# Conformer stage of a four-layer trunk: the whole depthwise convolution as 32x32 tiles on TensorE, modulation rows on VectorE

## The chip, the cores and the metric

The kernel runs on one core of a Trainium2 chip. The metric is the device time of one execution in microseconds (us), taken as the median of several runs. The engines are called as in the profile: PE is TensorE (PEld its weight loads), DVE is VectorE, ACT is ScalarE, POOL is GpSimd and SP is SyncE, which here issues the loads of weights.

## The reference, cut to what matters

A sequence of 256 tokens with 2048 channels passes four layers; the first one is a Conformer convolution module. Every sub-layer is gated and modulated by six vectors (shift, scale and gate of the mixer, then of the feed-forward network) that a per-layer projection, called adaLN, makes from one conditioning vector `c`.

```python
# each sub-layer f:  x <- x + gate * RMSNorm_post(f(RMSNorm_pre(x) * (1 + scale) + shift))
def _conv_module(h, w_in, dw_w, dw_b, ln_g, ln_b, w_out):
    a, gate = jnp.split(h @ w_in, 2, axis=-1)
    z = _causal_dwconv(a * jax.nn.sigmoid(gate), dw_w, dw_b)   # 31 taps for each channel
    z = jax.nn.silu(_layer_norm(z, ln_g, ln_b))
    return z @ w_out
```

All of it is in float32. The change touches only this module and the way in which the first layer's six modulation vectors are computed.

## The kernel before, in words

**Layout.** Channels lie on the 128 partitions, in 16 blocks (`KT` = 16, `P` = 128, `T` = 256 tokens). A matrix product in float32 is made of three products of a rounded part `hi` and a remainder `lo`: ACT writes `hi` (L121) and DVE writes `lo` (L123) for each weight. Weights arrive as items of 1 MB, 128x2048, in one list that SP loads in order.

**The input projection.** It runs in six steps, called s0 to s5 here, by the table `STEPS`: each takes some of the 16 input blocks (`nk` of them from `k0` on) for the output blocks `j0` to `j1`. Steps s0 to s2 add to all sixteen, s3 and s4 finish blocks 0 to 7, and s5 makes blocks 8 to 15 complete from eight input blocks. The matmuls are L756 to L758 (`ps_cin`). The function `gather` adds a result to `pair` (L665), and at a block's last step multiplies it by the sigmoid of its gate (L671).

**The convolution.** Eight blocks are convolved on DVE: 30 instructions each (L685), one per tap, two blocks at a time. The other eight (`PE_BLOCKS`) go over PE: four delayed copies of the block are made by matmuls with an identity (L713), copied out by ACT (L715), and 32 matmuls with diagonal weights add the taps (L730); the diagonals `zt` are made by DVE (L724) and ACT (L728), and ACT adds the bias (L733). The order in which these pieces are recorded is written out (`conv(dve, taps_dve, 8)` after each item of the last steps, then a loop over the rest).

**LayerNorm.** It runs over channels, that is over partitions. PE sums the blocks with a matrix of ones (L644 for the mean, L633 for the squares, one matmul of 128 columns for each block). DVE then forms `r_ln` (L783 to L786), takes the mean off all blocks (L789), multiplies each by `r_ln` (L792); ACT applies SiLU (L793), and the pair L424 and L425 splits the result into `uc`, the operand of the output projection (`ps_cout`, L522 to L524).

**Modulation.** A block of 128 values of a modulation vector can be made in two ways. As a *row*: DVE multiplies a 128x2048 item with the broadcast vector `cb` and sums along the line (L350). As *columns*: PE multiplies four items with `cz` (L364, 32 columns each, four tiles side by side in `ada`), DVE transposes the sums (L371) and PE adds them up (L378). Of the first layer's 96 blocks, 52 are made from columns before and 28 from rows, beside the 16 of the last gate, which come later, from rows, in both kernels. After the last step, 16 column items are used in the convolution's tail (`early_cols`) and some more in the output projection (`COLS_COUT`).

**What sets the order.** A scheduler puts the recorded instructions on each engine in an order that is then fixed; an engine runs its own in that order and waits at semaphores. `high_priority` and `issue_after` bend the order. Items wait in pools of four buffers: `raw` for weights and `cols` for early modulation items, and a load is issued when its buffer is free.

## Time and profile before

| what | value |
|---|---|
| median of 3 runs | 2378.56 us (2376.98 to 2380.26) |
| the profiled execution | 2376.87 us |
| its span, first to last instruction | 2375.2 us |
| granted clock of PE, mean | 0.992 |
| PE busy | 2318.7 us (98%) |
| DVE busy | 1772.2 us (75%) |
| ACT busy | 1212.4 us (51%) |
| DMA, mean | 256 GB/s over the span |

The profiled execution is 1.69 us below the median. The stages that the change touches end at about 466 us of the span: s0 begins at 29.6, s1 at 61.2, s2 at 95.1, s3 at 149.7, s4 at 183.7 and s5 at 211; the tail of the convolution runs from 266.7 to 352.4, LayerNorm up to 368.8, and the output projection up to 466.

A row of the table of windows gives the window, its length, then for PE, PEld, DVE, ACT and POOL the busy time and, in brackets, the number of instructions, then the granted clock, the share of DMA and its rate. A row of the timeline gives start, length, engine, operation and, in square brackets, the idle time before it with what ended it.

### The profile page before, as it was taken

The page shows a single profiled execution, that of the slowest core. Times are in us where ns is not written, and L with a number is a line of the kernel's source. Part 1 is how long each engine was busy: PE and PEld are TensorE (multiplying, and loading weights), DVE is VectorE, ACT ScalarE, POOL GpSimd, SP SyncE. Part 2 cuts the span into 40 slices and gives each one's busy share as a digit, 9 for nine tenths or more (in the row PEclk, how much of TensorE's full clock was granted, in tenths as well). Part 3 has the DMA queues.
Part 4 walks back from the last instruction along what each step waited for, and adds up shares of the span by engine and source line. Part 5 has one row for each costly group of instructions (what it writes and reads, how often), then busy time and mean ns, then how long its engine had stood idle before and what let it go on. Part 6 is the DMA issues. An engine that isn't in the chain of part 4 may idle for free.

```text
span 2375.2 us, 34238 instructions
## 1 busy us (share of the span) xinstructions
PE 2318.7 (98%) x13516; PEld 1955.8 (82%) x13516; DVE 1772.2 (75%) x2554; ACT 1212.4 (51%) x1909; POOL 16.8 (1%) x43
## 2 busy tenths in 40 slices
PE   6999998999999999999999999999999999999998
PEld 5888746788878888888878888888888888888886
DVE  3779998778878888888877877756887466645665
ACT  5334465555534554345565576655554455544543
POOL 0000000000000000000000000000000000000000
PEclk9999998999999999999999999999999999999999
DMA  9878778657799878988946756563778555555553
GB/s 387 344 311 322 299 222 309 265 216 276 291 310 348 303 279 316 362 288 298 345 174 258 283 216 227 168 227 121 286 280 275 193 190 193 189 185 196 193 199 121
DMA packets 86577, 609.30 MB, mean 257 GB/s; under 512 B 10064, under 2 KB 10128, under 8 KB 13456
## 3 DMA queue, kind: packets, MB, share of 16 engines
q1 hardware_dynamic: 84800, 601.84, 69.2%
q0 software_dynamic: 1472, 4.23, 0.6%
q8 instruction: 106, 1.74, 0.3%
q10 hardware_dynamic: 144, 1.05, 0.1%
q14 instruction: 55, 0.45, 0.1%
HBM read 604.94 MB, written 2.13 MB: 256 GB/s over the span
## 4 chain that ended last, share of the span: by engine, by line
PE 95%; DMA 2%; DVE 1%; ACT 1%; issue 0%; SPq 0%; DVEq 0%; ACTq 0%
PE ps_fb L410 14%; PE ps_fa L410 14%; PE ps_fa L412 7%; PE ps_fb L412 7%; PE ps_fo L524 7%; PE ps_fo L523 7%; PE ps_fo L522 6%; PE ps_cin L756 3%; PE ps_cin L758 3%; PE ps_r L410 2%; PE ps_cin L757 2%; PE ada L364 2%; PE ps_r L412 1%; PE ps_q L410 1%; PE ps_cout L522 1%; PE ps_k L410 1%
## 5 line engine op out<-in xcount | busy, mean ns | idle before, releaser
L123 DVE TENSOR_TENSOR lo<-raw,hi 128x1024 fp32r<-128x1024 f32 (+1 forms) x760 | 914.3, 1214 | 398.7 <-ACT hi L121 395.5
L121 ACT CAST hi<-raw 128x1024 fp32r<-128x1024 f32 (+1 forms) x760 | 784.9, 1042 | 807.4 <-PE ps_fa L410 195.4
L410 PE MATMUL ps_fa<-h,hi 128*128 128x512 f32 x1408 | 356.4, 393 | 0.4 <-ACT hn L486 0.4
L410 PE MATMUL ps_fb<-h,hi 128*128 128x512 f32 x1408 | 354.9, 392 | 0.0
L350 DVE CUSTOM_DVE_ANT_0 raw<-raw,cb 128x2048 f32<-128x2048 f32 x140 | 319.6, 2284 | 30.6 <-DMA raw<-in_adar 30.5
L410 PEld LDWEIGHTS ps_fa<-h,hi 128*128 128x128 f32 x1408 | 252.9, 189 | 45.7 <-DVE h L488 0.6
L410 PEld LDWEIGHTS ps_fb<-h,hi 128*128 128x128 f32 x1408 | 252.5, 189 | 44.2
L523 PE MATMUL ps_fo<-lo,u 128*128 128x512 f32 x704 | 274.6, 390 | 4.1 <-DVE lo L123 4.1
L524 PE MATMUL ps_fo<-hi,u 128*128 128x512 f32 x704 | 274.6, 390 | 0.0
L522 PE MATMUL ps_fo<-hi,u 128*128 128x512 f32 x704 | 273.7, 390 | 0.0
L412 PEld LDWEIGHTS ps_fa<-h,lo 128*128 128x128 f32 x1408 | 193.7, 190 | 15.1 <-DVE lo L123 0.5
L412 PEld LDWEIGHTS ps_fb<-h,lo 128*128 128x128 f32 x1408 | 193.7, 190 | 14.7
L412 PE MATMUL ps_fa<-h,lo 128*128 128x256 f32 x1408 | 198.3, 282 | 0.1
L412 PE MATMUL ps_fb<-h,lo 128*128 128x256 f32 x1408 | 198.2, 282 | 0.0
L523 PEld LDWEIGHTS ps_fo<-lo,u 128*128 128x128 f32 x704 | 132.6, 188 | 32.1 <-DVE lo L123 4.6
L756 PE MATMUL ps_cin<-h,hi 128*128 128x256 f32 x512 | 148.4, 293 | 7.3 <-ACT hi L121 7.2
L524 PEld LDWEIGHTS ps_fo<-hi,u 128*128 128x128 f32 x704 | 132.5, 188 | 27.7
L522 PEld LDWEIGHTS ps_fo<-hi,u 128*128 128x128 f32 x704 | 132.6, 188 | 27.1
L758 PE MATMUL ps_cin<-h,lo 128*128 128x256 f32 x512 | 145.2, 288 | 1.1 <-DVE lo L123 1.1
L757 PE MATMUL ps_cin<-h,hi 128*128 128x256 f32 x512 | 146.0, 287 | 0.0
L756 PEld LDWEIGHTS ps_cin<-h,hi 128*128 128x128 f32 x512 | 100.0, 196 | 21.5 <-ACT hi L121 11.8
L758 PEld LDWEIGHTS ps_cin<-h,lo 128*128 128x128 f32 x512 | 99.2, 196 | 3.2 <-issue 1.7
(240 smaller groups left out, 2697.9 us busy)
## 6 DMA issues: line engine op xcount, KB each, us to landing
raw<-in_fin SPq DMA_DIRECT2D x176, 1024.0 KB, 4.8
raw<-in_adar SPq DMA_DIRECT2D x140, 1024.0 KB, 5.6
raw<-in_fout SPq DMA_DIRECT2D x88, 1024.0 KB, 5.1
raw<-in_adac SPq DMA_DIRECT2D x44, 1024.0 KB, 5.8
raw<-in_gin SPq DMA_DIRECT2D x33, 1024.0 KB, 4.9
raw<-in_cin SPq DMA_DIRECT2D x32, 1024.0 KB, 11.1
raw<-in_cout SPq DMA_DIRECT2D x16, 1024.0 KB, 7.8
raw<-in_gv SPq DMA_DIRECT2D x16, 1024.0 KB, 4.8
```

The costliest lines, as they stand in the source:

```text
L121: nc.scalar.copy(hi[:, :w], r[:, s : s + w])
L123: nc.vector.tensor_sub(lo[:, :w], r[:, s : s + w], hi[:, :w].bitcast(F32))
L350: V.tensor_tensor_reduce(out=r, in0=r, in1=cb, scale=1.0, scalar=0.0, op0=ALU.mult, op1=ALU.add, accum_out=mod[l, m][:, k : k + 1])
L364: nc.tensor.matmul(ps[32 * (j % 4) : 32 * (j % 4) + 32], cz[:, kt], r[:, j * n : (j + 1) * n], start=kt < 4, stop=kt >= KT - 4, tile_posit ...
L410: nc.tensor.matmul(ps, hi(k * P), act[k], start=k == 0, stop=False)
L412: nc.tensor.matmul(ps[:, :T], lo(k * P), act[k][:, :T], start=False, stop=k == nk - 1)
L522: nc.tensor.matmul(pv, ah, wh, start=kt == 0, stop=False)
L523: nc.tensor.matmul(pv, ah, wl, start=False, stop=False)
L524: nc.tensor.matmul(pv, al, wh, start=False, stop=kt == nk - 1)
L756: nc.tensor.matmul(ps[:, b], hi(o), ah, start=k == 0, stop=False)
L757: nc.tensor.matmul(ps[:, b], hi(o), al, start=False, stop=False)
L758: nc.tensor.matmul(ps[:, b], lo(o), ah, start=False, stop=k == nk - 1)
```

## The change

**All sixteen blocks are convolved on PE.** For each tap and each quarter of the partitions stands one matmul of a 32x32 diagonal tile (`conv_taps`, L716 in the changed kernel): four quarters of rows times four groups of columns, so sixteen tiles, 124 matmuls in all for a block. The delay of a tap is an offset into `zp`, a copy of the block with 32 zeros ahead, so the delayed copies go. The four partial sums lie in four PSUM banks; ACT copies them out (L721), four matmuls add them up (`conv_sum`, L728) and ACT adds the bias (L729). The diagonals `zt` are made by DVE alone, two instructions of 128x512 for a block (L711). The convolution of a block is recorded after the projection of the next one (`LAG = 1`), and its sum one more block later.

**Statistics in fours.** Twelve of the sixteen blocks are summed four at a time into 32-row strips (`acc_p`, `acc_q`), and one more matmul adds up the strips.

**Modulation blocks.** 36 blocks move from columns to rows (16 from columns then, 64 from rows); one group of four stays for the gap (`gap_cols`). Rows of layer 0 take their buffers from the pool `cols`. Those recorded after LayerNorm are held behind its last instruction.

**LayerNorm.** Its DVE instructions are chained in a written order: three centerings, the reciprocal, and then for each block multiply, remainder and the centering of a later block.

**Loads at the start.** `cb` is loaded by SP instead of ACT, `par` comes in two parts, the table of taps is smaller (no scalar taps) and is loaded at s2.

```diff
-PE_BLOCKS = (5, 7, 9, 11, 12, 13, 14, 15)
+LAG = 1
-ADA = ((2, 1, 1, 0), (3, 3, 2, 0), (1, 1, 1, 1, 1, 1, 1, 1), (3, 3, 2, 0), (1,) * 4, (1,) * 8)
-COLS_CONV = 16
+ADA = ((2, 1, 1, 0), (3, 3, 2, 0), (1, 1, 2, 1, 2, 1, 2, 1), (3, 3, 2, 0), (3, 3, 3, 3), (2,) * 8)
+COLS = {4: (12, 16)}
-COLS_COUT = (0, 0, 0, 1), (1, 1, 1, 1), (1, 1, 0, 0), (0, 0, 0, 0)
-ROWS_COUT = (0, 0, 0, 4), (2, 1, 2, 1), (2, 1, 2, 1), (0, 0, 0, 0)
+ROWS_COUT = (1, 1, 1, 1), (1, 1, 1, 1), (1, 2, 1, 1), (0, 0, 0, 0)
...
-        early = key[0] == "col" or key[:3] in (("row", 0, 0), ("row", 0, 3))
+        early = key[0] == "col" or key[:2] == ("row", 0) and key[2] != 5
...
-    cols += [(0, m, k, 4, i) for m in (2, 4) for k in range(0, KT, 4) for i in range(4)]
-    rows += [(0, 3, k) for k in range(KT)]
+    cols += [(0, m, k, 4, i) for m in COLS for k in range(*COLS[m], 4) for i in range(4)]
+    rows += [(0, m, k) for m in (2, 3, 4) for k in range(KT) if m not in COLS or not COLS[m][0] <= k < COLS[m][1]]
...
-            V.tensor_tensor_reduce(out=r, in0=r, in1=cb, scale=1.0, scalar=0.0, op0=ALU.mult, op1=ALU.add,
-                                   accum_out=mod[l, m][:, k : k + 1])
+        with tc.issue_after(apool["ln"].ins) if "ln" in apool and l == 0 else ExitStack():
+            V.tensor_tensor_reduce(out=r, in0=r, in1=cb, scale=1.0, scalar=0.0, op0=ALU.mult, op1=ALU.add,
+                                   accum_out=mod[l, m][:, k : k + 1])
...
+            with tc.issue_after(apool["tok"].ins) if "tok" in apool else ExitStack():
+                nc.tensor.matmul(ps[32 * (j % 4) : 32 * (j % 4) + 32], cz[:, kt], r[:, j * n : (j + 1) * n],
+                                 start=kt < 4, stop=kt >= KT - 4, tile_position=(0, 32 * (j % 4)))
...
-                V.transpose(out=tr, in_=ps[:, h : h + T])
+                with tc.issue_after(apool["r"].ins) if "r" in apool else ExitStack(), tc.high_priority(SPLIT_FIRST):
+                    V.transpose(out=tr, in_=ps[:, h : h + T])
...
+            def conv_taps(j):
+                pss = [pp["ps"].tile([P, 2 * T], F32, tag="ps", name=f"ps_taps{j}_{b}")[:, :T] for b in range(4)]
+                for h in range(2):
+                    zt = cm.tile([P, 16, 32], F32, tag="zt", name="zt", bufs=2)
+                    V.tensor_mul(zt, tp[:, j, 16 * h : 16 * h + 16].unsqueeze(2).to_broadcast([P, 16, 32]),
+                                 mask32.unsqueeze(1).to_broadcast([P, 16, 32]))
+                    for d in range(16 * h, min(16 * h + 16, CW)):
+                        c = d % 4
                         for b in range(4):
+                            nc.tensor.matmul(pss[b][32 * c : 32 * c + 32], zt[32 * b : 32 * b + 32, d % 16],
+                                             zps[j % 3][32 * b : 32 * b + 32, 32 - d : 32 - d + T],
+                                             start=d < 4, stop=d + 4 >= CW, tile_position=(32 * b, 32 * c))
+                zc = cm.tile([P, 4, T], F32, tag="zc", name="zc")
+                for b in range(4):
+                    A.copy(zc[:, b], pss[b])
+                return zc
...
+            def conv_sum(j, zc):
+                ps = pp["ps"].tile([P, 2 * T], F32, tag="ps", name=f"ps_conv{j}")[:, :T]
+                for b in range(4):
+                    nc.tensor.matmul(ps[32 * b : 32 * b + 32], mask32, zc[:, b], start=True, stop=True, tile_position=(0, 32 * b))
+                A.activation(zs[j], ps, AF.Identity, bias=pc(C_DWB + j))
...
+                for j in range(3):
+                    center(j)
+                queue(V.reciprocal, r, r)
+                apool["r"] = line[-1]
+                for j in range(KT):
+                    queue(V.tensor_mul, zs[j], zs[j], r)
+                    A.activation(zs[j], zs[j], AF.Silu, bias=pc(C_LNB + j), scale=pc(C_LNG + j))
+                    us.append(hpool.tile([P, 2 * T], F32R, tag="h", name=f"uc{j}"))
+                    A.copy(us[j][:, :T], zs[j])
+                    low(j - 2)
+                    center(j + 3)
```

The next rows are the fixed order on DVE in step s4, between the completion of two neighbouring blocks. Before, L665 gathers a block, L685 is a tap of the convolution, L671 the product with the sigmoid and L123 a weight's remainder:

```order
L665 TENSOR_TENSOR pair_407<-pair_407,ps_cin_5_2096 128x512
L685 SCALAR_TENSOR_TENSOR pair_301<-pair_301,tp 128x247
L685 SCALAR_TENSOR_TENSOR pair_316<-pair_316,tp 128x247
L671 TENSOR_TENSOR pair_407<-pair_407,g 128x256
L685 SCALAR_TENSOR_TENSOR pair_301<-pair_301,tp 128x246
L685 SCALAR_TENSOR_TENSOR pair_316<-pair_316,tp 128x246
L685 SCALAR_TENSOR_TENSOR pair_301<-pair_301,tp 128x245
L685 SCALAR_TENSOR_TENSOR pair_316<-pair_316,tp 128x245
L685 SCALAR_TENSOR_TENSOR pair_301<-pair_301,tp 128x244
L123 TENSOR_TENSOR lo_0_2229<-raw_1970,hi_0_2228 128x1024
L123 TENSOR_TENSOR lo_1024_2233<-raw_1970,hi_1024_2232 128x1024
L685 SCALAR_TENSOR_TENSOR pair_316<-pair_316,tp 128x244
```

In the changed kernel the same place reads so (L697 gathers, L352 is a modulation row, `m_105` and `m_106` being its results, L702 the product with the sigmoid into `zp`, L711 a diagonal, L122 a weight's remainder); the first row is block 5 and the last one block 6:

```order
L697 TENSOR_TENSOR pair_411<-pair_411,ps_cin_5_2612 128x512
...
L122 TENSOR_TENSOR lo_1024_2800<-raw_2424,hi_1024_2799 128x1024
L702 TENSOR_TENSOR zp_183<-pair_411,g 128x256
L352 ISA raw_3579,m_106<-raw_3579,cb 128x2048
L352 ISA raw_3583,m_106<-raw_3583,cb 128x2048
L711 TENSOR_TENSOR zt<-tp,mask_91 128x512
L352 ISA raw_3795,m_106<-raw_3795,cb 128x2048
L711 TENSOR_TENSOR zt<-tp,mask_91 128x512
L352 ISA raw_3799,m_106<-raw_3799,cb 128x2048
L697 TENSOR_TENSOR pair_426<-pair_426,ps_cin_6_2803 128x512
```

The taps have gone from DVE, and rows stand in their place: 26 rows lie in s4 (none before), 11 in s2 (4 before), 8 in s3 (4 before), and none in s5. From the second gather of s2 to the gather of block 7 in s4 DVE has, in the changed kernel, 45 rows, 31 remainders, 31 gathers, 14 diagonals, 7 products with the sigmoid, 8 pairs that round `h`, and 8 small ones.

PE, at the end of the convolution, before the change (`ada` are column sums of modulation from an item `raw`, `acc_v` the sum of squares on which `r_ln` waits, `ps_cout` the output projection):

```order
L364 MATMUL ada_4160<-raw_3711,cz 32x512
L633 MATMUL acc_v<-sq_3835,ones 128x256
L364 MATMUL ada_4160<-raw_3711,cz 32x512
L633 MATMUL acc_v<-sq_3870,ones 128x256
L633 MATMUL acc_v<-sq_3875,ones 128x256
L364 MATMUL ada_4160<-raw_3711,cz 32x512 x2
L364 MATMUL ada_4160<-raw_4082,cz 32x512 x4
L522 MATMUL ps_cout_0_3992<-hi_0_4006,uc_3910 128x512
```

And in the changed kernel (L728 is the sum of the last block, 15):

```order
L728 MATMUL ps_conv_5077<-zc,mask_91 32x256 x4
...
L663 MATMUL acc_m<-pair_630,ones 128x256
L367 MATMUL ada_5216<-raw_4221,cz 32x512 x3
L367 MATMUL ada_5216<-raw_4223,cz 32x512
L663 MATMUL acc_v<-sq_5088,ones 128x256
L367 MATMUL ada_5216<-raw_4223,cz 32x512 x3
L663 MATMUL acc_v<-sq_5093,ones 128x256
L663 MATMUL acc_v<-sq_5097,ones 128x256
L367 MATMUL ada_5216<-raw_4431,cz 32x512
L663 MATMUL acc_v<-sq_5101,ones 128x256
L367 MATMUL ada_5216<-raw_4431,cz 32x512 x3
L367 MATMUL ada_5216<-raw_4433,cz 32x512 x4
```

Before, the column matmuls ahead of the last `acc_v` all use the item `raw_3711`, and the next item is used only behind it. Now the first matmul on a new item, `raw_4431`, stands ahead of the last `acc_v`, and SP issues that item's load only once the matmuls on `raw_4221` have run, since the load waits for PE to free a buffer of the pool `cols`; the load of `raw_4433` waits in the same way for `raw_4223`.

From the start of the first feed-forward network on, the order on every engine is the same in both kernels.

276 lines of the change are left out of this document (128 added, 148 removed).

## The prediction

> **What bounds the kernel now.** I read the table of windows first, one row per stage (window, length, busy PE, PEld, DVE, ACT and POOL with counts, granted clock, DMA share, GB/s).
>
> ```profile
> 95.10:149.70 54.60, 54.60 (x451) 49.43 (x450) 42.93 (x60) 20.11 (x22) 0.00 (x0) 1.00 0.80 319
> 149.70:183.70 34.00, 31.88 (x259) 27.61 (x258) 26.46 (x37) 10.12 (x13) 0.00 (x0) 0.95 0.88 356
> 183.70:211.00 27.30, 27.30 (x227) 23.88 (x225) 23.64 (x41) 13.73 (x20) 0.00 (x0) 1.00 0.92 370
> 211.00:266.70 55.70, 55.70 (x484) 48.34 (x480) 52.76 (x110) 21.37 (x30) 0.00 (x0) 1.00 0.67 263
> 266.70:352.40 85.70, 85.59 (x1054) 47.54 (x1048) 82.07 (x203) 51.04 (x182) 1.33 (x1) 1.00 0.73 264
> 352.40:368.80 16.40, 2.71 (x12) 0.20 (x8) 16.39 (x41) 7.92 (x15) 2.15 (x4) 0.68 0.94 200
> 368.80:466.00 97.20, 95.43 (x432) 75.30 (x428) 78.18 (x93) 50.69 (x80) 0.00 (x0) 0.98 0.79 310
> ```
>
> PE is busy all through s2, s4, s5 and the tail, but DVE is close behind: 43 of 54.6, 23.6 of 27.3, 52.8 of 55.7, 82 of 85.7. So there are two near-bounds, and what moves from one to the other matters more than what is removed. A busy PE is not a PE at its pitch, so I looked at starts of successive matmuls next.
>
> ```profile
> 222.13 0.28 PE L757 MATMUL ps_cin<-h,hi 128*128 128x256 f32 x1
> ...
> 223.69 0.28 PE L758 MATMUL ps_cin<-h,lo 128*128 128x256 f32 x1
> 223.90 0.24 PE L378 MATMUL adas<-adat,mask 128*32 128x2 f32 x8
> 224.07 0.39 PE L756 MATMUL ps_cin<-h,hi 128*128 128x256 f32 x1
> ...
> 306.22 3.23 PE L730 MATMUL ps_conv<-zr,zt 128*32 128x256 f32 x56
> ```
>
> Thirteen projection matmuls pass from 222.13 to 223.69, 0.12 us each; a block of s5 is 48 of them, 5.76 us, and a block of s4 24, 2.9 us. And 56 convolution matmuls with four column tiles side by side take 3.23 us; less the drawn length of the last one (0.38 in its group), 0.052 to 0.058 each, I take 0.0535.
>
> **What goes.** On DVE the 240 taps, a third of all its work in the last two stages; on PE the delayed copies and most column sums.
>
> ```profile
> 211.00:266.70 55.70, 28.59 (x71) 1.00 0.67 263
> 266.70:352.40 85.70, 58.88 (x151) 1.00 0.73 264
> ```
>
> These are L685 alone: 87.5 us of 134.8. The column matmuls (L364) have 29 us of the tail:
>
> ```profile
> 266.70:352.40 85.70, 29.03 (x142) 6.89 (x136) 1.00 0.73 264
> ```
>
> So s5 and the tail become much shorter. The order of the changed kernel shows where the price lies: rows stand in front, 11, 8 and 26 of them in s2, s3 and s4 (before 4, 4, 0), none in s5, and on DVE's fixed order each stands between gathers which PE needs.
>
> **The DVE list, s2 to the last gather of s4.** The prices, as busy time of a group over its count:
>
> ```profile
> 95.10:149.70 54.60, 9.14 (x8) 1.00 0.80 319
> ...
> L123 DVE TENSOR_TENSOR lo<-raw,hi 128x1024 fp32r<-128x1024 f32 x14 | 16.4, 1214 | 0.0
> L665 DVE TENSOR_TENSOR pair<-pair,ps_cin 128x512 f32<-128x512 f32 x10 | 6.6, 671 | 0.7 <-PE ps_cin L758 0.7
> ...
> L724 DVE TENSOR_TENSOR zt<-tp,mask 128x512 f32<-128x512 f32 x8 | 5.4, 675 | 0.0
> L671 DVE TENSOR_TENSOR pair<-pair,g 128x256 f32<-128x256 f32 x16 | 6.7, 417 | 0.1
> L488 DVE TENSOR_TENSOR h<-hn,h 128x256 fp32r<-128x256 f32 x32 | 12.8, 421 | 0.3
> L487 DVE CAST h<-hn 128x256 fp32r<-128x256 f32 x32 | 8.7, 290 | 3.3 <-ACT hn L486 3.3
> ```
>
> A row is 9.14/4 = 2.29 by itself. So: 45 rows 103.1; 31 remainders at 1.17, 36.3; 31 gathers at 0.66, 20.5; 14 diagonals at 0.675, 9.5; 7 products at 0.42, 2.9; 8 pairs for h at 0.67, 5.4; 8 small ones at 0.15, 1.2. Sum 179 us. In line they overlap, two rows start 2.21 apart:
>
> ```profile
> 420.26 2.28 DVE L350 CUSTOM_DVE_ANT_0 raw<-raw,cb 128x2048 f32<-128x2048 f32 x1
> ...
> 422.47 2.29 DVE L350 CUSTOM_DVE_ANT_0 raw<-raw,cb 128x2048 f32<-128x2048 f32 x1
> ...
> 424.69 2.35 DVE L123 TENSOR_TENSOR lo<-raw,hi 128x1024 fp32r<-128x1024 f32 x2
> ```
>
> At that, with 0.05 off each of the 99 other larger instructions, the list is 179 − 45 × 0.08 − 99 × 0.05 = 171 at the least. But the row of s5 shows DVE idle for 2.9 of 55.7 us even where it had most to do, and 171 × 55.7/52.8 is 180. I take 179, bounds 171 and 188 (waits of 8 at the first h tiles of stages). PE has less work in this stretch: in s4 a block costs 2.9 of projection and about 4.4 of convolution, while DVE has 13 to 19 us between two gathers. So DVE decides and PE waits about half of it. The list begins near 96 (s2 at 95.1, first gather and first h about 3 later, less 2 from the start, below) and ends at 96 + 179 = 275. Before, s4 ended at 211: **64 us later**.
>
> The start: the chain of waits has
>
> ```profile
> 25.45 0.57 DVE zt L724
> ...
> 27.15 1.48 ACT zt L728 x7
> ```
>
> there, which go: −2 (0 to −4, as other work may close the gap).
>
> **From there PE decides.** Left are 8 blocks of s5, ten sets of taps and ten sums. A set is 124 matmuls, recorded as 248 in the manner of the others (L730 has 64 records for 32). Before shows only four tiles side by side. If sixteen run at once, a set is 248 × 0.0535/4 = 3.3 us; if tiles of different rows take turns, 248 × 0.0535 = 13.3. I take 3.9, near the lower end, since four columns do run at once in the row above and nothing there binds rows differently; both ends are kept for the range. The Trainium skill ("TensorE: Matmul & The Clock Gate", Part 3: Packing small matmuls — row/col tiling) measured 10.6 times for sixteen such tiles at 512 columns; no run here shows it. By it a set would be an estimated 248 × 0.214/10.6 = 5.0 (0.214 being four of the 0.0535), and the sum below 11 us more.
>
> The switch of tile shape is priced by the rows above: the 32-column matmuls start 0.21 after the last wide one and the next wide one 0.17 later, against 0.12 without; 0.14 for a change there and back, 1.5 us in ten blocks. The Trainium skill ("TensorEngine Tiling (Array Packing)", Key Properties) says that a change of tiling mode drains TensorE; the trace agrees only in part, since the matmul at 223.69 lasts 0.28 and the next starts at 223.90, before its end at 223.97. By a full drain (0.16, what the last matmul still has to run, at three changes a block) I estimate 5 us more.
>
> Sum: 8 × 5.76 = 46; ten sets 39; ten sums 0.5 each, 5; the statistics, 3; stalls 3 (four of the six PSUM banks wait for ACT's copies, 0.39 each, which lie beside the next block's 5.8 us; up to 8 if not); the closing chain after the last sum (bias, mean, square, `acc_v`), 4. That is 100, from 275 to 375. DVE has 4.8 us for a block of s5 (two remainders, two diagonals, gather, product) and ACT about 5 (two casts, four copies, bias, sigmoid), both under PE's 10.2.
>
> **A wait that is added.** `raw_4431` can be loaded only after PE has used `raw_4221`, which is after block 15's sum; the last `acc_v` stands behind its first matmul, and behind that `r_ln`, all of LayerNorm and PE itself.
>
> ```profile
> raw<-in_adac SPq DMA_DIRECT2D x44, 1024.0 KB, 5.8
> ...
> 353.31 13.60 DMA raw<-in_adac
> ```
>
> 5.8 is the median from issue to landing, 13.6 the same kind of load at the same place before, with others in the queue. The last `acc_v` would else come some 2 us after the load is issued, when queues are quiet: about +6 (0 to 12). So `r_ln` at 381, against 352.4: +28.6.
>
> **LayerNorm and output projection.**
>
> ```profile
> 353.28 3.44 DVE L789 TENSOR_TENSOR pair<-pair,mu 128x256 f32<-128x256 f32 x10
> ...
> 356.64 1.75 DVE L786 RECIPROCAL r_ln<-r_ln 128x256 f32<-128x256 f32 x1
> 358.30 1.69 DVE L789 TENSOR_TENSOR pair<-pair,mu 128x256 f32<-128x256 f32 x5
> ...
> 366.96 1.94 PE L364 MATMUL ada<-raw,cz 128*32 128x512 f32 x8 [13.69 <-DMA raw<-in_adac]
> 368.83 0.80 PE L522 MATMUL ps_cout<-hi,uc 128*128 128x512 f32 x1
> ```
>
> The first projection matmul waited 13.69 for column items. That wait now lies ahead of `r_ln`; what is late next is the DVE chain: three centerings 1.0 (ten in 3.44), reciprocal 1.75, a transpose and a product 0.8, SiLU and cast 1, with its first two and the square root about 6, against 16.4. The projection then:
>
> ```profile
> 457.79 0.39 PE L523 MATMUL ps_cout<-lo,uc 128*128 128x512 f32 x1
> ...
> 462.78 0.40 PE L524 MATMUL ps_cout<-hi,uc 128*128 128x512 f32 x1
> 463.01 1.02 PE L551 MATMUL clock<-y,ident 128*128 128x512 f32 x2
> ```
>
> 22 steps in 4.99 us, 0.227 each, so its 384 matmuls need 87.2; before they took 94.2, from 368.83 to 463.01, with column sums between, and 3 more to 466. If PE never waits, the end is 6 + 87.2 + 3 = 96 after `r_ln`. But DVE works off LayerNorm beside it (16 blocks of three, 0.4 each, about 20 us) and then six held rows in a line (6 × 2.21 = 13.3) ahead of remainders that PE needs; PE has about one item of split weights in hand (24 matmuls, 5.4 us), so 8 of waits, and 1.5 at single remainders: 105.5. Against 113.6: −8 (−17 to −4). From the feed-forward network on nothing changes.
>
> **The sum.** +28.6 − 8 = +20.6 on the profiled execution's own 2376.87 (span 2375.2): 2397.5, rounded to **2398**; the median shown is 1.7 above that execution, which is inside the spread.
>
> **The rivals.**
> *DVE runs at its pitch* (not slower). I charged DVE idle time that it had in s5, and waits of PE for it in the projection. If it runs its list at the pitch of the two rows above, the list ends 8 us earlier, and the held rows are out of PE's way, the projection ending 96 after `r_ln` instead of 105: 2397.5 − 17 = 2381. It decides from where the list is under 171 us and the projection under 98. For it: a fixed list without releases in between has no reason to idle, and the rows are in buffers ahead; against it: gathers do wait for PE, remainders for ACT's casts, and DMA is at 0.8 to 0.9 of its time here. Chance 0.17, its times 2370 to 2387.
> *Tiles run eight at a time.* A set is 248 × 0.0535/2 = 6.6, and 7.2 with its ends: ten times 3.3 more, 2431. For it: the trace shows no more than four together, and a set has only four banks; against it: the four of the row share one bank already. Chance 0.13.
> *The change doesn't do what it says*: tiles of different rows take turns, 13.3 to 13.9 a set: +100, 2498. Chance 0.05. For it: no row shows tiles of different rows beside each other at all; against it: the tiles share neither rows, columns with the same bank, nor inputs.
> *Rows arrive late.* From 0 to the last gather of s4 about 87 items come in, at 2.8 us each by 370 GB/s 245 us, so 30 us to spare in all, but four buffers only, and a buffer's next load waits for DVE. Half a landing (2.8) at five blocks is +14, 2412. Chance 0.10.
> The forecast keeps 0.55, own range 2384 to 2412.
>
> **Chances.** A measurement of this kernel tells about 0.2% (4.8 us) from no change. Faster by more than that: 0.07, 0.04 of the first rival and 0.03 from the forecast's foot; within it: 0.11, 0.08 of the first rival and again 0.03; slower: 0.82, all the rest. The range reaches to 2372 below, which leaves out little of the first rival, and to 2434 above, with the eight tiles in; it leaves out the tiles that take turns and the ends of the others.
>
> **What would show it.** In the profile of the changed kernel: DVE without gaps from 96 to 275 and PE with 30 to 50% idle there; gathers of s4 13 to 19 us apart; then PE full and DVE half empty, blocks 10 us apart; `ps_taps` at 3.3 to 5 us a set; a wait for `raw` from `in_adac` of some 5 us just ahead of `r_ln`; the first `ps_cout` 6 us behind `r_ln`. The forecast is wrong if s4 ends much before 268, if a set takes over 6, or if the projection ends more than 110 us after `r_ln`.

## The result and the profile after

The changed kernel is slower: 2442.33 us (2439.93 to 2444.49, four runs) against 2378.07 us for the kernel before in the same job (2376.98 to 2380.26, four runs). The ratio is 1.0269, with an interval of 1.0251 to 1.0287. The profiled execution took 2439.93 us (span 2438.2), 63.06 more than that of before. The sign of the forecast was right; the time lies 44 us above it and outside its range.

The table of windows of the changed kernel, one row per stage from s2 on (window, length, busy PE, PEld, DVE, ACT and POOL with counts, granted clock, DMA share, GB/s). A stage ends at its last gather; the fifth row is the tail up to `r_ln`, the sixth LayerNorm, the last the output projection up to the first matmul of the feed-forward network:

```profile
93.90:152.10 58.20, 50.39 (x386) 49.40 (x386) 55.52 (x66) 16.47 (x18) 0.00 (x0) 0.94 0.90 354
152.10:188.70 36.60, 28.09 (x210) 27.48 (x209) 35.09 (x47) 9.87 (x13) 0.00 (x0) 0.91 0.84 345
188.70:287.40 98.70, 70.68 (x1741) 52.39 (x1751) 83.02 (x91) 22.62 (x47) 1.33 (x1) 0.84 0.94 345
287.40:390.40 103.00, 99.80 (x2476) 79.22 (x2490) 42.05 (x58) 36.68 (x77) 0.00 (x0) 1.00 0.26 92
390.40:420.40 30.00, 23.56 (x574) 11.46 (x574) 7.60 (x15) 11.40 (x25) 2.15 (x4) 0.95 0.42 143
420.40:426.80 6.40, 2.23 (x22) 0.49 (x22) 5.18 (x12) 3.12 (x6) 0.00 (x0) 0.98 0.65 236
426.80:535.80 109.00, 102.20 (x428) 79.67 (x429) 97.46 (x135) 59.80 (x102) 0.00 (x0) 0.95 0.68 259
```

Up to the end of s3 little has changed: with the same marks (a stage ends at its last gather) s3 ended at 184.0 before and ends at 188.7 now. From there to `r_ln` it was 168.4 us and is 231.7, and that is the whole loss. From `r_ln` to the feed-forward network it was 120.2 and is 115.4.

In s4 PE is busy for 70.7 of 98.7 us and DVE for 83.0. From the view of waits for s4 (engine, tile, line, what it waited for: us in total, times, longest):

```profile
DVE raw L352 <- DMA raw<-in_adar: 14.7, 4, 8.9
PE ps_taps L716 <- issue: 26.0, 7, 10.0
```

DVE waited for rows that had not been loaded, and PE waited in the middle of its sets of taps for nothing that the profile names. Each engine is thus full by itself: DVE's work and its waits for rows make 97.7 of the 98.7 us, PE's work and its waits of the kind "issue" 96.7, and they hardly wait for each other (PE 2.1 us for DVE, DVE 0.85 for PE, at the last gather). The chain of what ended last goes through the rows and their loads in s4 (shares of the stage; the view ends the line there):

```profile
by line: DMA raw<-in_adar 40.5%; DVE raw L352 30.5%; issue 7.3%; DVE lo L122 6.9%; DVE pair L697 3.6%; PE ps_taps L716 3.2%; DVE zt L711 2.6%; DVE zp L702 1.4%; PE ps_cin L766 1.2%; PE ps_cin L768 1.0%; PE ps_cin L767 1.0%; DVE m L352 0.7%;
```

The timeline of PE and DVE around the longest of these waits (start, length, engine, line, operation, idle time before it):

```profile
235.63 3.33 PE L716 MATMUL ps_taps<-zp,zt 32*32 32x256 f32 x142
...
248.98 4.33 PE L716 MATMUL ps_taps<-zp,zt 32*32 32x256 f32 x106 [10.03 <-issue]
250.53 2.29 DVE L352 CUSTOM_DVE_ANT_0 raw<-raw,cb 128x2048 f32<-128x2048 f32 x1 [8.91 <-DMA raw<-in_adar]
```

A set is recorded as 248 matmuls, and here PE stops after 142 of them, for 10 us, with both diagonals, the block and its banks at hand. Among the DMA packets of the trace are some of 16,384 bytes on the queue called "instruction". Laid beside the gaps in the taps of s4, in us (not a view of the profile, but read from the packets and the matmuls):

```
gap begins   packet begins   packet ends   PE goes on
  199.16        200.24          201.26       202.57
  213.29        214.24          215.12       216.53
  227.23        227.77          228.82       230.07
  238.58        245.58          248.11       248.98
  259.24        259.74          260.84       262.21
  264.62        265.89          267.05       268.41
  280.63        279.99          281.02       282.59
```

Each gap ends 0.9 to 1.6 us behind the end of such a packet. From the end of s3 to `r_ln` PE executes 4791 matmuls and as many weight loads by the rows above, and 37 packets come: 259 instructions to a packet. So "issue" reads here as PE waiting for its own instructions.

The longest wait of PE and the longest of DVE (10.0 and 8.9 us) lie in one stretch of slow loads. At 231.86 POOL had issued the transfer that writes the 2048 values of the mixer's gate to DRAM as a row (`row<-m`, 8.0 KB, 14.4 us to landing). Its row of the timeline, and the windows before, during and after the slow stretch:

```profile
231.86 1.33 POOL L516 DMA_DIRECT2D row<-m  x1 [229.68 <-DVE m L513]
```

```profile
224.00:236.00 12.00, 9.54 (x296) 6.87 (x296) 11.87 (x16) 3.41 (x8) 1.33 (x1) 1.00 1.01 416
237.00:247.00 10.00, 1.95 (x96) 1.24 (x89) 4.62 (x6) 0.42 (x1) 0.00 (x0) 0.81 1.06 111
249.00:260.00 11.00, 10.62 (x256) 7.42 (x255) 7.19 (x6) 2.68 (x6) 0.00 (x0) 0.80 1.02 425
```

The loads fall from 416 to 111 GB/s and come back to 425, while the share of DMA stays full. In the kernel before, POOL issues this transfer at 345.71, so that the slow stretch lies in LayerNorm, where PE waited 13.69 for column items:

```profile
352.00:362.00 10.00, 1.27 (x6) 0.14 (x4) 9.86 (x28) 4.97 (x9) 0.00 (x0) 0.82 0.91 71
```

By the packets, the loads of the changed kernel drop so behind each of its four transfers of this kind, from 357 to 416 GB/s down to 34 to 155. No run leaves the transfer out, so it is not shown to be the cause. What is shown is where it stands: the change brought it, and the slow stretch with it, from LayerNorm into s4.

### The profile page after: what moved, and what is told of

Its sections match the earlier page's. It is cut to its first block, busy times and chain, and to the rows that moved or that the text cites. A ratio compares the mean times of both kernels' runs of the same rounds, so it can differ in the third digit from the quotient of the medians.

```text
span 2438.2 us, 39779 instructions
## 1 busy us (share of the span) xinstructions
PE 2338.7 (96%) x16416; PEld 1983.3 (81%) x16416; DVE 1773.3 (73%) x2387; ACT 1194.4 (49%) x1809; POOL 16.8 (1%) x44
## 4 chain that ended last, share of the span: by engine, by line
PE 87%; DVE 6%; DMA 4%; issue 1%; ACT 1%; SPq 0%; DVEq 0%; ACTq 0%
PE ps_fb L416 13%; PE ps_fa L416 13%; PE ps_fa L418 7%; PE ps_fb L418 7%; PE ps_fo L531 6%; PE ps_fo L532 6%; PE ps_fo L530 6%; DVE raw L352 3%; DMA raw<-in_adar 3%; PE ps_r L416 2%; PE ps_taps L716 2%; DVE lo L122 2%; PE ps_cin L768 2%; PE ps_cin L766 2%; PE ps_cin L767 2%
## 5 line engine op out<-in xcount | busy, mean ns | idle before, releaser
L122 DVE TENSOR_TENSOR lo<-raw,hi 128x1024 fp32r<-128x1024 f32 (+1 forms) x760 | 915.9, 1215 | 425.9 <-ACT hi L120 420.8
L352 DVE CUSTOM_DVE_ANT_0 raw<-raw,cb 128x2048 f32<-128x2048 f32 x176 | 401.9, 2287 | 37.5 <-DMA raw<-in_adar 37.1
L418 PEld LDWEIGHTS ps_fb<-h,lo 128*128 128x128 f32 x1408 | 193.8, 191 | 14.7
L531 PEld LDWEIGHTS ps_fo<-lo,u 128*128 128x128 f32 x704 | 132.6, 188 | 31.8 <-DVE lo L122 4.4
L766 PE MATMUL ps_cin<-h,hi 128*128 128x256 f32 x512 | 152.7, 301 | 4.3 <-DVE h L496 2.3
L767 PE MATMUL ps_cin<-h,hi 128*128 128x256 f32 x512 | 150.3, 295 | 1.8 <-DVE h L496 1.8
L716 PE MATMUL ps_taps<-zp,zt 32*32 32x256 f32 x3968 | 93.1, 397 | 33.2 <-issue 31.0
```

The costliest lines, as they stand in the source:

```text
L122: nc.vector.tensor_sub(lo[:, :w], r[:, s : s + w], hi[:, :w].bitcast(F32))
L352: V.tensor_tensor_reduce(out=r, in0=r, in1=cb, scale=1.0, scalar=0.0, op0=ALU.mult, op1=ALU.add, accum_out=mod[l, m][:, k : k + 1])
L418: nc.tensor.matmul(ps[:, :T], lo(k * P), act[k][:, :T], start=False, stop=k == nk - 1)
L531: nc.tensor.matmul(pv, ah, wl, start=False, stop=False)
L716: nc.tensor.matmul(pss[b][32 * c : 32 * c + 32], zt[32 * b : 32 * b + 32, d % 16], zps[j % 3][32 * b : 32 * b + 32, 32 - d : 32 - d + T], ...
L766: nc.tensor.matmul(ps[:, b], hi(o), ah, start=k == 0, stop=False)
```

## The experiments

The measure in all of them is the time from the last gather of s3 to `r_ln`, in which the loss lies: 168.4 before, 231.7 after. At the end of this section stands a table. e2 to e6 and e9 were executed once each, the others four to ten times; executions of one kernel lie up to 11 us apart (e1), so a few us between two runs say nothing.

### e1: rows put where their loads are ready

```diff
-        with tc.issue_after(apool["ln"].ins) if "ln" in apool and l == 0 else ExitStack():
+        gate = apool.get("ln") or (apool.get("zp") if m in (2, 3, 4) else None) if l == 0 else None
+        with tc.issue_after(gate.ins) if gate else ExitStack():
...
-                    V.tensor_mul(zps[j % 3][:, 32:], Y[j][:, 0], g)
+                    apool["zp"] = V.tensor_mul(zps[j % 3][:, 32:], Y[j][:, 0], g)
```

(`zp` is the last product into `zps`; rows of s4 are so held behind products and spread into s5.)

> The modulation rows of layer 0 that are not needed inside the stage (scale, gate and shift of the later sub-layers) are held behind the product of the block at which they are recorded, so that they stand about three for every two blocks of s4 and two for each block of s5 instead of 26 in s4. Theory A, rows in front of gathers on DVE's fixed order make PE wait, and the loads that they need in so short a time make it worse: the last gather of s4 comes about 40 us earlier than 287, s5 stays bound by PE, and the time falls by 40 to 50 us to about 2395. Theory B, the stage is bound by the bytes to be loaded, whatever their order: only the 15 us of waits for loads go, about 2425.

Measured 2438.81 us, ratio 1.0256 [1.0237, 1.0275]. Both theories missed. The windows of its s4, s5 and tail:

```profile
190.50:273.00 82.50, 66.67 (x1740) 51.36 (x1753) 45.94 (x56) 22.39 (x47) 0.00 (x0) 0.92 0.53 206
273.00:392.40 119.40, 105.29 (x2476) 80.50 (x2486) 78.45 (x94) 36.67 (x77) 1.33 (x1) 0.97 0.60 222
392.40:422.60 30.20, 23.52 (x574) 11.40 (x573) 7.59 (x15) 11.39 (x25) 2.15 (x4) 0.93 0.43 142
```

17 of the 26 rows left s4, which became 16 us shorter, and s5 became 16 longer with DVE at 78 of 119. DVE's list alone does not set the time: with half of it gone from s4 the sum stays, and PE's matmuls alone need 189 of the 232 us (counted as in the part on the prediction).

### e2 and e3: rows without their loads, and without their time on DVE

```diff
-            self.nc.sync.dma_start(out=r[:, : it["n"]], in_=it["src"])
+            if not (it["kind"] == "row" and it["key"][1] == 0 and it["key"][2] != 5):
+                self.nc.sync.dma_start(out=r[:, : it["n"]], in_=it["src"])
...
-            V.tensor_tensor_reduce(out=r, in0=r, in1=cb, scale=1.0, scalar=0.0, op0=ALU.mult, op1=ALU.add,
+            V.tensor_tensor_reduce(out=r, in0=cb if l == 0 and m != 5 else r, in1=cb, scale=1.0, scalar=0.0, op0=ALU.mult, op1=ALU.add,
```

> Leaves out: the loads of layer 0's modulation rows (the rows read the broadcast vector twice, in the same time on DVE). The order on DVE stays near that of the changed kernel. Theory A (DVE's list bounds s2 to s4): the last gather of s4 comes at 270 to 276 instead of 287, and the time is 2420 to 2430. Theory B (loads bound it): the gather comes before 250, time below 2405. If PE's stalls without a shown reason in s4 (26 us) come from instruction loads that queue behind the rows' loads, they go to a few us; if not, they stay.

Measured 2447.49 us. Neither theory came: the last gather of s4 stood at 293.7, later than with the loads. Order and waits changed: PE waited 17.4 us for diagonals, while the waits of its taps of the kind "issue" fell from 31.0 to 11.3. So this run can't price the loads cleanly; it shows that taking them away gains nothing.

```diff
-            V.tensor_tensor_reduce(out=r, in0=r, in1=cb, scale=1.0, scalar=0.0, op0=ALU.mult, op1=ALU.add,
+            w = 128 if l == 0 and m != 5 else D
+            V.tensor_tensor_reduce(out=r[:, :w], in0=r[:, :w], in1=cb[:, :w], scale=1.0, scalar=0.0, op0=ALU.mult, op1=ALU.add,
```

> Leaves out: most of each modulation row of layer 0 on DVE (128 of 2048 columns are multiplied and summed; all loads stay). Theory A: without some 90 us of DVE the last gather of s4 comes where PE or the loads put it, at 235 to 250, and the time is 2390 to 2405. Theory B: it stays behind the loads, 265 or later, time above 2418.

Measured 2420.47 us, with the last gather of s4 at 270.3, which is theory B. s3 ended 13.8 us earlier, at 174.9, but from there s4 still took 95.4. DVE's view of waits for this stretch, and its window, show what came in place of its work:

```profile
DVE raw L353 <- DMA raw<-in_adar: 46.8, 18, 13.5
```

```profile
174.90:270.30 95.40, 70.76 (x1735) 50.92 (x1741) 33.24 (x91) 22.53 (x47) 1.33 (x1) 0.89 1.00 372
```

The loads of the rows take the time that the rows themselves had taken: DMA is busy throughout, at 372 GB/s. (PE's waits for instructions, 22.7 us here, fill PE's side of the stage as before.)

### e4, e5, e6: fewer instructions, fewer columns

e4 leaves out the taps of the second half (64 matmuls for a block, in place of 124). e5 keeps the matmuls but gives each half of the tokens. e6 has e4's 64 matmuls, each with 512 columns.

```diff
 e4, e6
-                for h in range(2):
+                for h in range(1):
-                                             start=d < 4, stop=d + 4 >= CW, tile_position=(32 * b, 32 * c))
+                                             start=d < 4, stop=d + 4 >= 16, tile_position=(32 * b, 32 * c))
 e5
-                            nc.tensor.matmul(pss[b][32 * c : 32 * c + 32], zt[32 * b : 32 * b + 32, d % 16],
-                                             zps[j % 3][32 * b : 32 * b + 32, 32 - d : 32 - d + T],
+                            nc.tensor.matmul(pss[b][32 * c : 32 * c + 32, : T // 2], zt[32 * b : 32 * b + 32, d % 16],
+                                             zps[j % 3][32 * b : 32 * b + 32, 32 - d : 32 - d + T // 2],
 e6
-                                             zps[j % 3][32 * b : 32 * b + 32, 32 - d : 32 - d + T],
+                                             zps[j % 3][32 * b : 32 * b + 32, 32 - d : 32 - d + T].unsqueeze(1).to_broadcast([32, 2, T]),
```

> Leaves out: taps 16 to 30 of the convolution (64 instead of 124 tile matmuls for a block, one diagonal instruction instead of two). If s5 and the tail are bound by PE and a set of taps costs by its number of matmuls (5.2 us now), a set takes 2.7, blocks of s5 come every 9.6 instead of 12.2 us, and the time falls by about 25 us to 2415. If blocks of s5 wait for something else (ACT's copies, the gather, loads), the pitch stays above 11 and the time within 10 us of 2440.

> Leaves out: the convolution of tokens 128 to 255 (each tap matmul has 128 columns instead of 256; number and order of instructions stay). Theory I, a set of taps is limited by how its 248 matmuls and 248 weight loads come to PE (issue, and the loading of instructions by DMA in 16 KB packets): a set stays at 4.5 us or more, PE's stalls without a shown reason stay above 15 us, and the time is within 20 us of 2442. Theory S, it is limited by streaming columns through the tiles: a set falls to about 3 us and the time to 2390 to 2400, as with half of the taps (2385).

> Leaves out: taps 16 to 30, and streams the 256 tokens twice through each of the others (512 columns), so that there are half as many instructions with as many columns in all as in the changed kernel. Theory I: as with half of the taps, 2385 to 2395. Theory S: a set takes about 5 us again and the time is above 2420.

Measured: 2385.45, 2435.7 and 2422.23 us. The group of the taps on PE, from s4 to the end of the convolution, in the changed kernel, e4, e5 and e6 (count, busy us, mean ns, idle time before and what ended it):

```profile
L716 PE MATMUL ps_taps<-zp,zt 32*32 32x256 f32 x3968 | 93.1, 397 | 33.2 <-issue 31.0 <-DVE zt L711 1.2 <-DVE zp L702 0.9
```

```profile
L716 PE MATMUL ps_taps<-zp,zt 32*32 32x256 f32 x2048 | 48.3, 400 | 5.3 <-issue 4.1 <-DVE zp L702 1.3
```

```profile
L716 PE MATMUL ps_taps<-zp,zt 32*32 32x128 f32 x3968 | 67.8, 301 | 43.3 <-issue 42.4 <-DVE zp L702 0.9
```

```profile
L716 PE MATMUL ps_taps<-zp,zt 32*32 32x512 f32 x2048 | 77.5, 612 | 3.0 <-issue 1.2 <-DVE zp L702 0.9 <-ACT zc L721 0.8
```

The waits follow the number of matmuls: 31 and 42 us with 3968 records, 4 and 1 with 2048. Half the columns alone saves 6.6 us: PE is busy 25 us less with taps and waits 11 more. Half the instructions at the same columns saves 20, both together 57. That e5 and e6 add up to 27 and e4 gives 57 says that one limit hides the other, but the order changed too: s4 is 70.0 us in e4, with 18 rows in it, while e6, with all 26, still needs 95.3 there. The window of e6's s4 and its waits:

```profile
189.40:284.70 95.30, 64.61 (x1020) 44.03 (x1035) 79.46 (x86) 21.74 (x47) 1.33 (x1) 0.84 0.95 347
```

```profile
DVE raw L352 <- DMA raw<-in_adar: 15.8, 6, 8.6
PE ps_cin L766 <- DVE pair L697: 27.7, 5, 13.2
```

With PE's waits for instructions gone, DVE's 79.5 us of work and 15.8 of waits for rows fill the stage, and PE waits for DVE. So in s4 the waits for instructions cost the changed kernel no more than the 3.4 us by which e6 is shorter. In e5 it is the other way round: with 20 rows in s4, PE's 66.0 of work and 26.5 of waits for instructions fill the 93.4 us, and DVE waits for PE. That is why the time of e5 fits theory I and the time of e6 theory S: neither tests one limit by itself. s5 and the tail shrink in both, from 103.0 and 30.0 to 92.0 and 26.2 in e6, and to 82.7 and 22.8 in e4.

### e7: modulation blocks made as before

The tables `ADA`, `COLS_COUT` and `ROWS_COUT` and the lists `cols` and `rows` of before, with three items a block in s5; the convolution and LayerNorm as changed.

```diff
-    cols += [(0, m, k, 4, i) for m in COLS for k in range(*COLS[m], 4) for i in range(4)]
-    rows += [(0, m, k) for m in (2, 3, 4) for k in range(KT) if m not in COLS or not COLS[m][0] <= k < COLS[m][1]]
+    cols += [(0, m, k, 4, i) for m in (2, 4) for k in range(0, KT, 4) for i in range(4)]
+    rows += [(0, 3, k) for k in range(KT)]
```

> The modulation blocks as before the change (52 from columns, 28 from rows), with three column items in each block of s5, beside the new convolution, statistics and LayerNorm. If the rows in s2 to s4 are the main cause of the loss, the last gather of s4 comes 35 us earlier, and the time is at or below 2405. If the taps on PE are (16 sets of over 5 us, and stalls for instructions), s4 stays near 85 us long, and the time is 2425 to 2445.

Measured 2443.33 us, ratio 1.0275 [1.026, 1.029]. Its windows of s4, s5 and tail:

```profile
181.90:250.30 68.40, 62.81 (x1768) 46.92 (x1780) 27.42 (x38) 20.90 (x46) 0.00 (x0) 1.00 0.42 167
250.30:360.60 110.30, 108.11 (x2588) 81.81 (x2587) 43.33 (x62) 35.28 (x73) 0.00 (x0) 1.00 0.44 165
360.60:414.90 54.30, 43.58 (x722) 14.95 (x722) 12.06 (x30) 12.45 (x29) 3.49 (x5) 0.94 0.97 317
```

The last gather of s4 came 37 us earlier, as the first of the two cases said, and the time is in the range of the second. Not one row is left in s4, DVE is busy for 83 of 233 us, and the stretch takes 233.0 against 231.7. The move of the modulation blocks, from PE to DVE, changes nothing in the sum: what s4 gains, s5 and the tail lose, with the columns back on PE. The loss comes with the convolution: DVE lost the taps and nobody needed that.

### e8 and e11: the parts put into the kernel before

e8 is the kernel before with the changed LayerNorm alone (chain in written order, L783 to L796 replaced).

```diff
+            with tc.high_priority(SPLIT_FIRST):
+                queue(V.scalar_tensor_tensor, part_a, acc["m"], 1.0 / D, part_a, ALU.mult, ALU.add)
...
+                for j in range(3):
+                    center(j)
+                queue(V.reciprocal, r, r)
+                for j in range(KT):
+                    queue(V.tensor_mul, zs[j], zs[j], r)
...
+                    low(j - 2)
+                    center(j + 3)
```

> The kernel before with one part of the change alone: LayerNorm's written order on DVE (three centerings, reciprocal, then block by block), with the column matmuls held behind the output projection's and the transposes behind the reciprocal. The wait of 13.7 us for column items ahead of the first projection matmul goes: that matmul 6 to 7 us after r_ln instead of 16.4, and a time of 2366 to 2370. If the held rows and columns then make the projection longer by as much, 2374 to 2378.

Measured 2381.59 us, ratio 1.0018 [1.0008, 1.0028], above both cases. The timeline of its first projection matmul, with the wait before it:

```profile
358.96 0.80 PE L525 MATMUL ps_cout<-hi,uc 128*128 128x512 f32 x1 [6.31 <-ACT uc L817]
```

It follows `r_ln` by 6.3 us, against 16.4 before. But from `r_ln` to the feed-forward network it is 122.4, against 120.2: the ten us are given back in the projection. The windows from 400 to 440 of e8 and of the kernel before show it:

```profile
400.00:440.00 40.00, 34.13 (x155) 23.93 (x154) 35.64 (x36) 8.64 (x12) 0.00 (x0) 0.91 0.98 394
```

```profile
400.00:440.00 40.00, 40.00 (x193) 30.29 (x193) 37.69 (x40) 16.41 (x18) 0.00 (x0) 1.00 0.94 371
```

The loads run at 0.98 there and PE has fewer matmuls, which fits weights that set the pace; no run tested it.

e11 is the kernel before with sixteen small tiles in place of the four delayed copies, for its eight blocks on PE; the other eight stay on DVE.

```diff
-                            nc.tensor.matmul(pr4[32 * i : 32 * i + 32], ident[:, 32 * b : 32 * b + 32], zp[:, 4 - i : 32 + T - i],
-                                             start=True, stop=True, tile_position=(0, 32 * i))
...
-                            nc.tensor.matmul(ps[32 * b : 32 * b + 32], zt[:, a % 4, b], zr[:, b, 28 - 4 * a : 28 - 4 * a + T],
-                                             start=a == 0, stop=a == 7, tile_position=(0, 32 * b))
+                                nc.tensor.matmul(pss[b][32 * c : 32 * c + 32], zt[32 * b : 32 * b + 32, i],
+                                                 zp[32 * b : 32 * b + 32, 32 - d : 32 - d + T],
+                                                 start=k < 4, stop=k + 4 >= CW, tile_position=(32 * b, 32 * c))
...
+                        nc.tensor.matmul(ps[32 * b : 32 * b + 32], mask32, zr[:, b, :T], start=True, stop=True, tile_position=(0, 32 * b))
```

> The kernel before with one part of the change alone: its eight blocks on PE are convolved with sixteen tiles and no delayed copies; the other eight stay on DVE, and statistics, LayerNorm and modulation are as before. If the loss comes from giving all sixteen blocks to PE (PE's own sum from the last gather of s3 to r_ln is 187 us against 168), eight sets at 5.6 us with their sums against 6.0 us for copies and taps change little: 2370 to 2385. If the tiles' many short instructions are the loss by themselves, whatever the number of blocks, PE shows stalls of over 15 us and the time is above 2395.

Measured 2424.55 us, ratio 1.0194 [1.0176, 1.0212]. Its group of taps in the tail, from the last gather at 266.9 to `r_ln` at 408.0:

```profile
L719 PE MATMUL ps_taps<-zp,zt 32*32 32x256 f32 x1984 | 53.3, 437 | 24.6 <-DVE zt L714 14.7 <-issue 9.0 <-DVE m L381 0.9
```

That tail is 141 us, against 85.8. Without gaps the taps and their sums need 49.2 + 8.5 on PE for eight blocks, against 47.7 for the delayed copies and the convolution that they replace. Most of the rest are waits, 31.5 us by PE's busy time: 14.7 for diagonals, two buffers of which are all there are (DVE waits 22.3 us for PE to free one), and 12.9 for instructions, 3.9 of them at column matmuls. That is the second case. So the tiles are dearer on PE than what they replace even when only half the blocks use them.

### e9 and e10: the wait ahead of `r_ln`

e9 gives the last four squares a buffer each; e10 does so and leaves no column group for the gap (`COLS = {}`, its four blocks as rows).

```diff
-                    sq = cm.tile([P, T], F32, tag=f"sq{i}", name=f"sq{j}", bufs=1)
+                    sq = cm.tile([P, T], F32, tag=f"sq{j % 4}", name=f"sq{j}", bufs=1)
 e10 also
-COLS = {4: (12, 16)}
+COLS = {}
-ROWS_COUT = (1, 1, 1, 1), (1, 1, 1, 1), (1, 2, 1, 1), (0, 0, 0, 0)
+ROWS_COUT = (1, 1, 1, 2), (1, 2, 1, 2), (1, 2, 1, 2), (0, 0, 0, 0)
```

> One edit to the changed kernel: the squares of the last four blocks go to four buffers instead of one, so that each need not wait for the sum of the one before (1.66 us apart in its trace). From the last gather of s5 to r_ln 27 us instead of 30; the first load of the gap's columns still ends last, so that part may not fall at all: 27 to 30, time 2438 to 2443.

> The same, and the four column items of the gap become four rows in the output projection. My forecast put the wait for the item ahead of the last acc_v at 6 us (0 to 12): then 21 to 24 us from the last gather of s5 to r_ln, and a time of 2432 to 2437. If the load only hides the serial squares, 26 and 2438.

Measured 2439.55 us (e9), and 2442.32 us, ratio 1.0275 [1.026, 1.0291] (e10). From the last gather of s5 to `r_ln` the changed kernel takes 30.0 us, e9 21.5, e10 21.4. So ahead of `r_ln` the column item's load costs only while the squares share a buffer. But in e9 the wait for it has moved: PE waits 5.3 us for column items behind `r_ln`, and the first projection matmul follows by 10.9 instead of 6.4. In e10 it follows by 6.3, and the projection then takes 10.5 longer. From `r_ln` to the feed-forward network it is 120.5 in e9 and 125.8 in e10, against 115.4, so most of the 8.5 us, and all of it in e10, is given back. The view of waits for e10's projection:

```profile
PE ps_cout L528 <- ACT hi L120: 12.2, 1, 12.2
PE ps_cout L528 <- ACT uc L816: 6.4, 1, 6.4
```

### All runs side by side

The runs by the marks that they have in common, in us (worked out from starts in the timelines of the profiled execution; the time is the median):

| kernel | last gather of s3 to `r_ln` | of it s4, s5, tail | `r_ln` to feed-forward | time |
|---|---|---|---|---|
| before | 168.4 | 31.8, 50.8, 85.8 | 120.2 | 2378.07 |
| after | 231.7 | 98.7, 103.0, 30.0 | 115.4 | 2442.33 |
| e1 rows spread | 232.1 | 82.5, 119.4, 30.2 | 115.7 | 2438.81 |
| e2 rows without loads | 241.8 | 108.9, 101.3, 31.6 | 115.4 | 2447.49 |
| e3 rows short on DVE | 228.4 | 95.4, 102.6, 30.4 | 110.6 | 2420.47 |
| e4 half the matmuls | 175.5 | 70.0, 82.7, 22.8 | 115.4 | 2385.45 |
| e5 half the columns | 225.8 | 93.4, 101.4, 31.0 | 116.9 | 2435.7 |
| e6 half the matmuls, double columns | 213.5 | 95.3, 92.0, 26.2 | 114.6 | 2422.23 |
| e7 modulation as before | 233.0 | 68.4, 110.3, 54.3 | 122.6 | 2443.33 |
| e9 squares apart | 224.4 | 98.7, 104.2, 21.5 | 120.5 | 2439.55 |
| e10 no columns in the gap | 225.0 | 99.2, 104.4, 21.4 | 125.8 | 2442.32 |
| e8 before, changed LayerNorm | 168.6 | 33.1, 49.2, 86.3 | 122.4 | 2381.59 |
| e11 before, sixteen tiles | 223.7 | 31.8, 50.8, 141.1 | 112.8 | 2424.55 |

Where rows, columns and squares stand moves time between s4, s5 and the tail, and leaves the sum at 224 to 242 (e1, e2, e3, e7, e9, e10). Only less work in the taps themselves takes it far below. No version tried beats the kernel before.

## Why the prediction was right in sign and wrong in size

**Right.** The start gave −3.9 by the beginning of s2 (forecast −2). DVE's list of s2 to s4 was priced at 179: from the first gather's mark to the last one of s4 it took 190.7, with 170.8 of work, 14.7 of waits for loads and 4.0 for PE. So DVE does decide there. The first `ps_cout` follows `r_ln` by 6.4 (forecast 6). What was called a rival with a chance of 0.10, that rows arrive late at +14, came true with 14.7, and since the list itself was on time, the last gather of s4 came 12.4 behind the forecast's 275. The size of that rival was luck: it was made of five half landings, and 8.9 of the 14.7 are one wait, in the slow stretch behind `row<-m`, which the forecast did not see. Nor did it see that the landing of 13.60, which it put down to others in the queue, lay largely in the same stretch of the kernel before.

**The step that failed: "I take 3.9, near the lower end".** The price of a set of taps was mis-sized, by more than any other term. The timeline shows a clean set of s5 from 300.78 to 306.0, 5.2 us, and the chain of what ended last (start, length) agrees:

```profile
300.85 5.14 PE ps_taps L716 x216
```

Over all sixteen sets it is 4.96, if only steps below 0.5 us from one tap to the next are counted, and the ten sets behind s4 need 5.3 each with their ends, as counted below. By the pitch of four tiles, 13.3 us for four at a time, 5.14 is an estimated 10.3 tiles at once: the rival of turns didn't come, and the truth lies between the forecast's sixteen (3.3) and the rival of eight (6.6 to 7.2). I had divided the pitch of four tiles by four, the best case, and added 0.6. The Trainium skill ("TensorE: Matmul & The Clock Gate", Part 3: Packing small matmuls — row/col tiling) gave 10.6 times, by which the prediction had estimated 5.0; the trace agrees with it, at 5.14. At half the columns a set still needs 3.55 (e5, counted like the 4.96), so part of the price hangs on the matmul and not on its columns.

**Wrong: statistics at 3.** They take 9.2 behind s4, 5.0 for the last four blocks and 4.2 for the strips; the prediction gave no working for its 3. The column sums of the gap had no term at all.

The whole of the stretch that PE decides, from the last gather of s4 to `r_ln`, by the terms of the forecast (each matmul from its start to the next one's start; a step above 0.55 us counted as 0.25 and a gap):

| term | forecast | measured |
|---|---|---|
| projection, 8 blocks | 46 | 48.2 |
| ten sets of taps | 39 | 52.8 |
| ten sums | 5 | 6.0 |
| statistics | 3 | 9.2 |
| column sums | 0 | 3.2 |
| stalls, closing chain, wait for the load | 13 | 13.6 |
| sum | 106 | 133 |

That is 27 us, of which the sets of taps have 13.8, the statistics 6.2 and the column sums 3.2; blocks of s5 come about 12 us apart, not 10. With the 12.4 of s4, and 3.2 since LayerNorm and projection gave −4.8 instead of −8, it makes 42.6, and the profiled execution was 42.4 above the 2397.5.

**Right by another reason than I thought: the wait ahead of `r_ln`.** The timeline of the tail (SPq is SP's issue of a load):

```profile
410.05 1.95 SPq L96 DMA_DIRECT2D raw<-in_adac  x2
...
417.29 1.92 PE L367 MATMUL ada<-raw,cz 128*32 128x512 f32 x2 [3.33 <-DMA raw<-in_adac]
419.14 1.22 PE L663 MATMUL acc_v<-sq,ones 128*128 128x256 f32 x2
420.40 0.42 DVE L790 SCALAR_TENSOR_TENSOR r_ln<-acc_v,part_a 128x256 f32<-128x256 f32 x1 [5.97 <-PE acc_v L663]
```

The load is there, 7.2 from issue to use, and `r_ln` waits 6. But e9 keeps the load and loses 8.5 us here by the squares' buffers, and e10, without the load, no more. Wait and buffers were one chain, of which I had seen one half.

**Right in part: "PE has less work in this stretch ... So DVE decides and PE waits about half of it."** DVE decides, by the chain of s4, and the work of PE leaves 31 us of the 98.7 free. But PE spends 26.0 of them waiting for instructions and only 2.1 waiting for DVE, so it was not the spare engine that the forecast took it for.

**Why the change loses.** Counted in the same way from the last gather of s3 to `r_ln`, and without any gap, PE's matmuls need 168.6 us before and 187.3 after: the convolution went from 47.7 (copies included) to 97.8 (88.7 of taps and 9.1 of sums), the statistics fell from 17.0 to 9.7, and the columns from 32.7 to 3.2. The projection, the same work, took 5.4 more (76.6 against 71.2). So the change takes 29.5 and 7.3 us from PE and gives it 50.1, on the engine that had no gaps there before. Even without a gap the stretch would be 18.7 us longer than before; on top come 44.6 us of gaps, 31 of them in s4. e7 shows that giving the blocks of modulation back doesn't help: with no row in s4 the stretch is 233 us, 211 of work on PE and 21.5 of gaps. (The prediction calls the taps a third of DVE's work in the last two stages; its own lines give 87.5 of 134.8 us, about two thirds. Its sum doesn't use that.)

**What the forecast had no term for: PE's instructions.** 26 of the 98.7 us of s4 are "issue". They explain little of the miss, since DVE and its rows fill s4 as well (e6), and behind s4 they are 5 us. They go with the number of instructions (e4, e6 against e5) and, as far as the runs tell, with the load on DMA: in the changed kernel 26 of 31 us lie in s4, at a DMA share of 0.94, and 5 behind it, at 0.26 to 0.42; with the rows' loads taken away (e2) it is 11.3, with modulation as before (e7, share 0.42 and 0.44 in s4 and s5) 8.0. The Trainium skill ("Runtime: NRT & Kernel Launch", Instruction fetch mechanics) describes the supply: blocks of 16 KiB, 256 instructions, fetched by the sequencer's own queue while it executes. The packets here agree, with 259 to a packet; that its cost is "mostly hidden" holds for the kernel before, where PE has no such gap in these stages, and not for this one, with 31 us.

**Open.** In s4 two chains of nearly one length stand side by side, rows with their loads and PE with its waits for instructions: taking one limit away (e2, e3, e6) leaves the next at 95 to 109 us, and e2 changed the order as well. A supply of instructions made faster with all the work kept wasn't tried, nor a kernel without `row<-m` in s4. The projection's matmuls in s4 take 28.4 without gaps, where the forecast's price makes 23, at a granted clock of 0.84; they take 24.0 at 1.00 (e7), 25.5 at 0.92 (e1) and 30.4 at 0.78 (e5), which fits the clock, though e10 has 25.3 at 0.85.

## What to carry to other kernels

Before work is moved off an engine that is second, add up what the first one gets in exchange, in its own time: here DVE lost 87.5 us of taps, and PE, which was the bound, got 50 us of convolution for 37 of relief. Packing small tiles multiplies instructions; count them beside the columns, price a set from the nearest measured pitch without the best case, and look for "issue" waits in runs of short matmuls. Where work is fed by loads, count the loads of the stage beside the work (e3: DMA at 1.00), and ask which small transfers the new order brings into it. An earlier start counts only if what feeds the next stage comes earlier too: twice (e8, e10) an earlier start of the output projection was given back inside it.

## What the runs showed of the hardware

Packets of PE's instructions never begin closer together than 3.2 to 3.4 us where sets of taps run (after 3.33, e1 3.35, e2 3.23, e5 3.39, e7 3.32), while in the kernel before none are closer than 7.4. A set has 496 instructions, matmuls and weight loads, so by 259 to a packet and 3.3 us each its supply takes an estimated 6.3 us, more than the 4.96 in which PE executes it; a set of 64 matmuls needs about 3.3, less than e6's 4.15. That fits runs with 31 to 42 us of waiting and runs with 1 to 4, but it isn't the whole. In e4 a clean set is executed in 2.7 us, less than 3.3, and its taps wait only 4.1 in all. In s4 of the changed kernel packets begin 5.9 to 11.9 us apart, and five of the seven at its waits begin 0.5 to 1.3 us after PE has stopped. How far ahead PE fetches the trace doesn't show. One packet in s4 began 7.0 us after PE had stopped and took 2.5 instead of 0.9 to 1.2, in the slow stretch behind `row<-m`, in which a row's load too came 8.9 us late.

In all thirteen traces the loads slow down for some ten us behind each `row<-m` of 8 KB: from 6 to 14.5 us after its issue they come at 13 to 182 GB/s, and packets of 8 KB that took 0.31 us take up to 6.2 (s4 of the changed kernel). Ahead of it they come at 329 to 419, but for one place each in the kernel before, e2, e8 and e11, where few loads run there.

A matmul's price in such a set does not follow its columns alone: counted by steps below 0.5 us, 128, 256 and 512 columns gave 3.55 us for 124 matmuls, 4.96 for 124, and 4.15 for 64, which is 29, 40 and 65 ns for each.
